# Memory keys of layer 1 moved into the first expert stage of a two-block fp32 transformer on one core, score copies put ahead of exponentials, key transposes put later

## The chip, the cores and the metric

The kernel runs on one core of one Trainium2 chip, in one launch. The metric is device time in microseconds (us); three runs of the kernel before gave a median of 1918.88 us (1917.76 to 1919.21). The engines are named as in the profile: PE (TensorE matmul), DVE (VectorE), ACT (ScalarE), POOL (GpSimd), SP (SyncE, which here starts nearly all weight transfers).

## The reference, cut to what matters

Everything is fp32. Two blocks of two layers each run one after the other. The first block works on 256 rows of width 1024:

```python
for layer in range(2):
    mix = even_mixer(x, ...) if layer % 2 == 0 else odd_mixer(x, ...)   # sliding window + spatial gate | pooling
    x = layer_norm(ALPHA * x + mix, ln1_g, ln1_b)
    x = layer_norm(ALPHA * x + memory_cross_attention(x, mem, xq, xkv, xo), ln2_g, ln2_b)
    x = layer_norm(ALPHA * x + grouped_moe(x, router_w, router_bias, e_gate, e_up, e_down), ln3_g, ln3_b)

def memory_cross_attention(x, mem, wq, wkv, wo):
    q = (x @ wq)...; kv = (mem @ wkv)...; k, v = kv[:, :, 0], kv[:, :, 1]     # mem: 256 rows, known from the start
    p = softmax(q k^T * X_HEAD_DIM ** -0.5); return (p v) @ wo

def grouped_moe(...):                     # 16 experts, two of them picked for each row
    he = silu(xt @ w_gate[e]) * (xt @ w_up[e]); y += combine[:, e:e+1] * (he @ w_down[e])
```

The second block (layers with adaptive norms, whose factors are rows `ada` made from a conditioning vector) has in layer 0 a differential attention (two softmaxes for each head, the second subtracted with a factor) and a SwiGLU network, and in layer 1 a grouped-query attention with normed and rotated queries and keys, and a second SwiGLU network.

The memory's keys and values for layer 1 (`mem @ wkv`) depend on nothing but inputs, so they can be formed at any time before the cross attention of layer 1.

## The kernel before, in words

**Arithmetic.** A large fp32 product is made from three matmuls on split operands. A weight chunk is 1 MB (128x2048). Its two halves of 128x1024 are each cast on ACT to `wh` (L253), and DVE or POOL subtracts to get the remainder `wl` (L254); `W.lo` names the engine of each half. The matmuls are hi x hi, lo x hi, hi x lo (L339 to L341, or L389 to L391 where the weight is the stationary operand). Expert weights (`gate`, `up`, `down`) are not split: they go raw into single matmuls (L1208, L1219).

**Weight stream.** The class `Stream` (object `W`) holds the planned order of all chunks. `load` starts transfers on SP's queue, in that order, as long as a buffer of some kind is free. The kinds and counts stand in `W.spare`: `raw`, and idle buffers of others (`w` is a pair of `wh`/`wl` buffers, `big` a large tile, `x`, `q`). `fill` gives a chunk to its user, and where it is not a raw one it writes the two casts and two subtractions at that place of the program. `ahead` calls `fill` for chunks further down the order, as far as free room goes, so the place of a cast on ACT is set by where `ahead` is called and by how many buffers there are.

**Order.** Each engine runs its instructions in the order in which the Python code emits them; there is no other scheduler. What is late on one engine holds what is emitted behind it.

**First expert stage, `moe(0)`.** The 16 experts run as eight pairs p. In step p the loop forms `gate` of pair p (four chunks), transposes the hidden rows of pair p-1 (`hidden_T`), adds the product of pair p-2 to its rows (`back`, matmuls `sct`, L1123 and L1124, operands `oh` and `ol`), forms `up` of pair p, calls the pair's hook, and runs `down` of pair p-1, whose product `po` is split on ACT and DVE into `oh` and `ol` (`out_split`). In step 8 the hook loads the transposed memory (`load_mem`, tile `memT`). After the stage, `last` adds the last pair, the layer norm is run, and in its gaps PE forms the four key chunks of layer 1 (`mem_k(1, j)`, tiles `memk` to `memK`, 48 matmuls of 128x256 each) and two halves of `ada` (`ada_go`). `W.spare["big"]` is 3 in the later pairs.

**Cross attention of layer 1.** The two value chunks of the first half (`mem_v(1, 0)`, 48 matmuls of 128x512 on `memv`) lie in the gaps of `w_out1`; those of the second half (`mem_v(1, 1)`) are the fill between the scores and the products of `cross`.

**Differential attention.** Each of 32 units (one head and one row tile) goes through `scores` (`dsc`, maximum `dmx` on DVE L1617 and L1618, two exponentials on ACT L1622), `combine` (DVE), `turn` (PE transposes L1639, ACT copy L1640) and `values` (PE `po` L1648). A `step(u)` runs the scores of unit u, one of its fills (half of a weight chunk's matmuls, `qkvp`), the `turn` of unit u-1, a second fill, and the values of unit u-1.

**Grouped-query attention.** `kv_tile` forms keys and values of a row tile (`gkv`), their square sums are turned to factors on POOL (`gkr`, L2004 and L345 to L356), `k_turn` scales on DVE (L2034) and transposes on PE (L2038), `q_half` forms queries (`gq`).

Of the kernel before, what the change touches and what calls it, by code (L numbers as in the profile page):

```python
# [213 lines left out]
def _build(nc, tc, A, out, ctx, order, plan):  # L214
# [601 lines left out]
    def mem_v(l, nh, vm):  # L816

        pss = [mm([128, 512], f"memv{t}") for t in range(2)]
        for i in range(2):
            ws = W.get(f"xv{l}", 2 * nh + i)  # L820
            W.ahead()
            tm_half(pss, range(2), fmt(memh), fmt(meml), ws, 4 * i, 8)
            if i == 1:
                for t in range(2):
                    S.copy(vm[:, t, nh * 512:nh * 512 + 512], pss[t])
            yield

    def idle():
        pass

    def mem_v_steps(l, vm):
        step = mem_v(l, 0, vm)
        return (lambda: next(step)), idle, (lambda: next(step))

    kT = big([128, 8, 256], F32, "memK")
# [96 lines left out]
    def cross(l, x, xh, xl, kT, vm, mid):  # L932
# [40 lines left out]
        for h in range(4):  # L973
            ps = mm([128, 2, 256], "xo", "B")
            for i in range(2):
                j = 2 * h + i
                for mc in range(2):
                    T.matmul(ps[:, i], vm[:, mc, j * 128:j * 128 + 128], PT[:, mc, h], start=mc == 0, stop=mc == 1)
            split(oh[:, 2 * h:2 * h + 2], ol[:, 2 * h:2 * h + 2], ps)
        return add_ln_router(l, x, f"xo{l}", fmt(oh), fmt(ol), f"ln2_{l}")  # L980

# [124 lines left out]
    def gated(pg, pu, cgc):  # L1106
        sg, hm = s2([128, 512], F32, "sg"), s2([128, 512], F32, "hm")
        S.activation(sg, pg, AF.Silu)
        V.scalar_tensor_tensor(hm, pu, cgc, sg, op0=OP.mult, op1=OP.mult)
        return hm  # L1110
# [82 lines left out]
    def moe(l, x, hooks):  # L1193
# [52 lines left out]
        for p in range(9):  # L1246
            if p == 1:
                W.spare["big"] = 1
            if p == 5:
                W.spare["big"] = 3  # L1250
            if p == 8:
                W.spare.update(w=0, big=0, x=1 - l, q=1 - l)
                W.lo = V, G
            if p < 8:
                pg = first(p, "gate")
            if p == 0:
                gains(0)
            else:
                hT[p - 1] = hidden_T(hm.pop(p - 1))
            if p > 1:  # L1260
                back(p - 2, 0)
            if p < 8:
                pu = first(p, "up")
                hm[p] = gated(pg, pu, cg[:, p:p + 1])
            if p == 0:
                ada_end()
                affine(0)
            if p == 1:
                affine(1)
                lists_T(0)  # L1270
            if p in (2, 3):
                gather_half(1, range(4 * p - 8, 4 * p - 4), "BB")
            if p == 3:
                gains(1)
                lists_T(1)
            if p > 1:
                back(p - 2, 1)
            if p == 4:
                beyond_lists()
            if p in hooks:  # L1280
                hooks[p]()
            if p:
                o[p - 1] = down(p - 1, hT.pop(p - 1))
# [2 lines left out]


    vm = big([128, 2, 1024], F32, "memV")
    x, xh, xl = add_ln(0, x, "w_out0", fmt(mh), fmt(ml), "ln1_0", *mem_v_steps(0, vm), mid=gate_T)
    W.spare.update(x=1, q=1)  # L1290
    W.whole, W.lo = 4, (V, G)
    x = cross(0, x, xh, xl, kT, vm, mem_v(0, 1, vm))

    def late_mem():
        nonlocal memh, meml, kT
        memh, meml = load_mem(G)
        yield
        kT = big([128, 8, 256], F32, "memK")
        for j in range(4):
            mem_k(1, j, kT)  # L1300
            if j % 2:
                ada_go()
            yield

    mk = late_mem()
    last, tt = moe(0, x, {8: lambda: next(mk)})
    W.whole = 4
    gb = ln_gb(2, "ln3_0")
    for t in range(2):
# [66 lines left out]
            V.scalar_tensor_tensor(ml[:, k], ps[:, i], sc, mh[:, k].bitcast(F32), op0=OP.mult, op1=OP.subtract)  # L1376
    ada_go()
    W.ahead()
    vm = big([128, 2, 1024], F32, "memV")
    W.spare["x"] = 0  # L1380
    x, xh, xl = add_ln(3, x, "w_out1", fmt(mh), fmt(ml), "ln1_1", *mem_v_steps(1, vm))
    W.spare.update(x=1, q=1)
    x = cross(1, x, xh, xl, kT, vm, mem_v(1, 1, vm))

    xs4 = [None] * 4
    order4 = (2, 3, 0, 1)
# [211 lines left out]
    class Unit:  # L1598
# [7 lines left out]
        def scores(self):  # L1606
# [5 lines left out]
            for m, ps in enumerate(pss):  # L1612
# [3 lines left out]
                mm3(ps, *q, *k, True, True)  # L1616
                V.tensor_reduce(mx[:, m:m + 1], ps, axis=AX, op=OP.max)  # L1617
            V.scalar_tensor_tensor(mx, mx, -1.0, rq, op0=OP.mult, op1=OP.mult)  # L1618
            self.P = []
            for m in range(2):  # L1620
                P = s2([128, 512], F32, "dP")
# [227 lines left out]
    def step(u, fills):  # L1849

        fills = list(fills)

        def fill():
            if fills:
                fills.pop(0)()

        if u < len(units):
            units[u].scores()
        out_step()
        if len(fills) > 1:  # L1860
            fill()
        if u:
            units[u - 1].turn()
        Qs[-1].scale(1)
        if u < len(units):
            units[u].combine()
        if 2 < u < 27:
            W.ahead(2)
        fill()
        Qs[-1].turn(1)  # L1870
        if u:
            units[u - 1].values()
# [180 lines left out]
    tabs = next(rope)  # L2053
    gate = [gate_row(1, 0, 0)]
    kv_tile(0)
    k_turn(1)
    kv_tile(1)
    W.limit = 2
    W.ahead()
    qs, qss, rq, pq = {}, {}, {}, {}  # L2060
# [28 lines left out]
    for i in range(2):  # L2089
        for t in range(2):  # L2090
            q_half(0, i, t)
            if i:
                q_heads(0, t)
        if i == 0:
            k_turn(0)
    for t in range(2):
        q_half(1, 0, t)
        q_turn(0, t)
    os_ = []
    Pg, PTs = {}, {}  # L2100
# [103 lines left out]
```

## Time and profile before

| | us |
|---|---|
| median of three runs | 1918.88 |
| the profiled execution, device time | 1917.83 |
| its span, first to last instruction | 1916.1 |
| PE busy in it | 1819.1 |
| DVE, ACT, POOL busy | 974.7, 703.8, 369.9 |
| mean granted TensorE clock | 0.984 of full speed |

The page's chain of work that ended last gives PE 59%, DMA 12%, DVE 9%, ACT 4% of the span. The stages differ: in the expert stages the DMA engines move about 421 GB/s with a busy share at or just over 1, elsewhere they move 56 to 320 GB/s. A busy time of PE in the expert stages counts matmuls that wait in the pipeline, so 19 of 20 us there do not say that PE is full.

### The profile page before, as it was taken

To read this page: it belongs to the slowest core of one execution; us is meant where nothing else is said; L and a number is where in the kernel's file an instruction comes from. 1 tells how busy PE (TensorE), PEld (TensorE's weight loads), DVE (VectorE), ACT (ScalarE), POOL (GpSimd) and SP (SyncE) were. 2 spreads that over 40 slices of the span, in tenths; PEclk is the share of its full clock that TensorE was granted. 3 is DMA by queue.
4 is the path that set the end of the run, shared out by engine and by line. 5 is a ranking of instruction groups with operands and counts; after the bars stand their busy time and mean duration, and the time that the engine had idled before them with its cause. 6 is when DMAs were issued, how large, how long until landed. Compare 5 with 4: busy or idle time off the path is not lost.

```text
span 1916.1 us, 25646 instructions
## 1 busy us (share of the span) xinstructions
PE 1819.1 (95%) x10038; PEld 1331.5 (69%) x10038; DVE 974.7 (51%) x1731; ACT 703.8 (37%) x1212; POOL 369.9 (19%) x594
## 2 busy tenths in 40 slices
PE   7999899999999899998899999999999998899998
PEld 6988634336788534335798876778888876559997
DVE  6884511115694421116666666534343466756665
ACT  6654312004554312103544543422322234545442
POOL 0003000003353000204575653100000024410000
PEclk9999899999999899999999999999999999999999
DMA  7546799999755899997511122342324223464552
GB/s 267 207 170 228 292 414 422 421 422 390 285 210 190 326 415 421 421 422 311 200 56 67 67 88 89 110 146 96 132 100 142 97 81 106 176 233 167 184 189 97
DMA packets 81587, 424.22 MB, mean 221 GB/s; under 512 B 9408, under 2 KB 9856, under 8 KB 49200
## 3 DMA queue, kind: packets, MB, share of 16 engines
q1 hardware_dynamic: 78768, 409.66, 56.2%
q0 software_dynamic: 2688, 12.81, 1.8%
q8 instruction: 83, 1.36, 0.3%
q14 instruction: 48, 0.39, 0.1%
HBM read 421.35 MB, written 1.08 MB: 220 GB/s over the span
## 4 chain that ended last, share of the span: by engine, by line
PE 59%; DMA 12%; DVE 9%; ACT 4%; issue 2%; POOL 2%; ACTq 0%; DVEq 0%; SPq 0%; POOLq 0%
DMA spare<-down 4%; DMA spare<-up 3%; PE fg L1702 3%; PE fu L1704 3%; PE fu L1703 3%; PE fu L1702 3%; PE fg L1703 3%; PE fg L1704 3%; PE fd L341 3%; PE fd L340 3%; PE fd L339 3%; PE pu L1208 3%; PE pg L1208 3%; DMA spare<-gate 3%; PE po L1219 2%
## 5 line engine op out<-in xcount | busy, mean ns | idle before, releaser
L253 ACT CAST wh<-raw 128x1024 fp32r<-128x1024 f32 (+1 forms) x248 | 248.5, 1047 | 131.0 <-PE fd L341 90.5
L254 DVE TENSOR_TENSOR wl<-raw,wh 128x1024 fp32r<-128x1024 f32 (+1 forms) x192 | 239.6, 1282 | 86.6 <-ACT wh L253 86.4
L254 POOL TENSOR_TENSOR wl<-raw,wh 128x1024 fp32r<-128x1024 f32 x56 | 144.5, 2594 | 252.8 <-ACT wh L253 241.8
L1703 PE MATMUL fg<-f,wh 128*128 128x256 f32 (+1 forms) x360 | 120.6, 335 | 2.6 <-DVE f L1435 2.4
L1702 PE MATMUL fg<-f,wh 128*128 128x256 f32 (+1 forms) x360 | 121.1, 336 | 1.7 <-DVE f L1434 1.4
L1702 PE MATMUL fu<-f,wh 128*128 128x256 f32 (+1 forms) x360 | 120.5, 335 | 0.0
L1703 PE MATMUL fu<-f,wh 128*128 128x256 f32 (+1 forms) x360 | 120.5, 335 | 0.0
L1704 PE MATMUL fu<-f,wl 128*128 128x256 f32 (+1 forms) x360 | 120.4, 334 | 0.0
L1704 PE MATMUL fg<-f,wl 128*128 128x256 f32 (+1 forms) x360 | 120.0, 333 | 0.0
L1219 PE MATMUL po<-spare,hT 128*64 128x512 f32 x456 | 109.1, 598 | 6.6 <-DMA spare<-down 2.3
L339 PE MATMUL qkvp<-wh,h 128*128 128x256 f32 x384 | 112.8, 294 | 0.5 <-ACT qsq L1560 0.5
L1721 DVE TENSOR_TENSOR fsg<-fu,fsg 128x512 f32<-128x512 f32 (+1 forms) x44 | 24.5, 558 | 171.1 <-PE fu L1704 169.2
L340 PE MATMUL qkvp<-wl,h 128*128 128x256 f32 x384 | 109.2, 284 | 1.8 <-POOL wl L254 1.8
L341 PE MATMUL qkvp<-wh,h 128*128 128x256 f32 x384 | 108.9, 284 | 0.0
L339 PE MATMUL fd<-wh,hid 128*128 128x512 f32 x264 | 103.0, 390 | 0.0
L340 PE MATMUL fd<-wl,hid 128*128 128x512 f32 x264 | 102.8, 389 | 0.0
L341 PE MATMUL fd<-wh,hid 128*128 128x512 f32 x264 | 102.7, 389 | 0.0
L1208 PE MATMUL pg<-spare,xg 128*64 128x512 f32 x360 | 87.1, 596 | 3.9 <-DMA spare<-gate 3.7
L253 ACT CAST hid<-fsg 128x512 fp32r<-128x512 f32 (+1 forms) x44 | 22.6, 513 | 183.5 <-DVE fsg L1721 183.5
L1208 PE MATMUL pu<-spare,xg 128*64 128x512 f32 x360 | 87.0, 597 | 0.4 <-DMA spare<-up 0.4
L253 ACT CAST oh<-po 128x512 fp32r<-128x512 f32 x32 | 18.7, 585 | 183.9 <-PE po L1219 183.9
L1219 PEld LDWEIGHTS po<-spare,hT 128*64 128x64 f32 x456 | 35.0, 136 | 73.1 <-issue 48.9
(667 smaller groups left out, 4272.2 us busy)
## 6 DMA issues: line engine op xcount, KB each, us to landing
spare<-down SPq DMA_DIRECT2D x94, 512.0 KB, 11.1
raw<-gu SPq DMA_DIRECT2D x42, 1024.0 KB, 4.9
spare<-up SPq DMA_DIRECT2D x80, 512.0 KB, 12.3
raw<-ada SPq DMA_DIRECT2D x36, 1024.0 KB, 5.1
spare<-gate SPq DMA_DIRECT2D x62, 512.0 KB, 11.1
raw<-dn SPq DMA_DIRECT2D x22, 1024.0 KB, 4.9
raw<-gate SPq DMA_DIRECT2D x19, 1024.0 KB, 12.3
raw<-up SPq DMA_DIRECT2D x19, 1024.0 KB, 13.5
```

The costliest lines, as they stand in the source:

```text
L253: (H.tensor_copy if H else S.copy)(hi, src)
L254: E.tensor_sub(lo, src, hi.bitcast(F32))
L339: T.matmul(ps, sh, mh, start=start, stop=False)
L340: T.matmul(ps, sh, ml, start=False, stop=False)
L341: T.matmul(ps, sl, mh, start=False, stop=stop_)
L1208: T.matmul(ps[64 * s:64 * s + 64], xg[h][k // 4][:, k % 4, 128 * b + 64 * s:128 * b + 64 * s + 64], w[s][:, kk * 512:kk * 512 + 512], star ...
L1219: T.matmul(po[nh][64 * s:64 * s + 64], hT[:, k, 64 * s:64 * s + 64], w[s][:, nh * 512:nh * 512 + 512], start=k == 0, stop=k == 3)
L1702: T.matmul(ps[:, cs], hi[:, c], h_, start=k == 0, stop=False)
L1703: T.matmul(ps[:, cs], hi[:, c], l_, start=False, stop=False)
L1704: T.matmul(ps[:, cs], lo[:, c], h_, start=False, stop=k == 7)
L1721: V.tensor_tensor(sg[:, :n], pss[1][:, :n], sg[:, :n], op=OP.mult)
```

## The change

It has three parts. First, the hook of steps 4 to 8 of `moe(0)` is now one step of `late_mem` each: the memory is loaded in step 4, the key tile taken in step 5, and key chunks 0, 1 and 2 formed in steps 6, 7 and 8; chunk 3 and both halves of `mem_v(1, 0)` follow after the stage, with `ada_go` beside them. `W.spare` has other counts there, remainders go to DVE (`W.lo = V, V`), and `W.fill(W.used + 1)` is called ahead of `gated` in the later steps and in step 8. The gaps of `w_out1` now take `mem_v(1, 1)`, the fill of the cross attention is four halves of `ada`, and since `ada` work is thereby earlier, the last four calls of `ada_go` (after `gout`) find nothing to do. Second, the exponentials leave `scores` and stand in a method `exps`, called behind the `turn` of the unit before. Third, `kv_tile(1)` runs ahead of `k_turn(1)`, and `k_turn(0)` behind `q_half(1, 0, 0)`.

```diff
     def mem_v_steps(l, vm):
-        step = mem_v(l, 0, vm)
+        step = mem_v(l, l, vm)
...
         for p in range(9):
             if p == 1:
                 W.spare["big"] = 1
+            if p == 4 and l == 0:
+                W.spare["w"], W.lo = 3, (V, V)
             if p == 5:
-                W.spare["big"] = 3
+                W.spare["big"] = 1 if l == 0 else 3
             if p == 8:
                 W.spare.update(w=0, big=0, x=1 - l, q=1 - l)
                 W.lo = V, G
+                if l == 0:
+                    W.fill(W.used + 1)
...
                 pu = first(p, "up")
+                if l == 0 and p > 4:
+                    W.fill(W.used + 1)
                 hm[p] = gated(pg, pu, cg[:, p:p + 1])
...
     def late_mem():
-        nonlocal memh, meml, kT
+        nonlocal memh, meml, kT, vm
         memh, meml = load_mem(G)
         yield
         kT = big([128, 8, 256], F32, "memK")
         for j in range(4):
+            yield
             mem_k(1, j, kT)
-            if j % 2:
-                ada_go()
+        yield
+        vm = [q4([128, 1024], F32, "memV") for _ in range(2)]
+        step = mem_v(1, 0, vm)
+        next(step)
+        yield
+        next(step)
+        for _ in range(3):
+            ada_go()
             yield

     mk = late_mem()
-    last, tt = moe(0, x, {8: lambda: next(mk)})
+    last, tt = moe(0, x, {p: lambda: next(mk) for p in range(4, 9)})
...
-    x = cross(1, x, xh, xl, kT, vm, mem_v(1, 1, vm))
+    def ada_fill():
+        for _ in range(2):
+            ada_go(2)
+            yield
+
+    x = cross(1, x, xh, xl, kT, vm, ada_fill())
...
             V.scalar_tensor_tensor(mx, mx, -1.0, rq, op0=OP.mult, op1=OP.mult)
+            self.pend = pss, mx, rq
+
+        def exps(self):
+            n, (pss, mx, rq) = 128 * self.nk, self.pend
             self.P = []
...
         if u:
             units[u - 1].turn()
+        if u < len(units):
+            units[u].exps()
         Qs[-1].scale(1)
...
     kv_tile(0)
+    kv_tile(1)
     k_turn(1)
-    kv_tile(1)
...
-        if i == 0:
-            k_turn(0)
     for t in range(2):
         q_half(1, 0, t)
+        if t == 0:
+            k_turn(0)
         q_turn(0, t)
```

**ACT at the end of the first expert stage.** This is ACT's queue before, from the product of pair 5 to the first key chunks (`wh<-spare` x6 are key chunks 0 to 2, two halves each; po_3690 is the product of pair 6, po_3755 that of pair 7).

```order
L253 CAST oh<-po_3567 128x512
L253 CAST oh<-po_3568 128x512
L1103 COPY hT<-tp 128x512
L1108 ACTIVATE sg<-pg 128x512
L253 CAST oh<-po_3690 128x512
L253 CAST oh<-po_3691 128x512
L1103 COPY hT<-tp 128x512
L253 CAST memTh<-spare 128x512 x4
L253 CAST oh<-po_3755 128x512
L253 CAST oh<-po_3756 128x512
L253 CAST wh<-spare 128x1024 x6
```

And this is the same queue of the changed kernel (po_3630 is the product of pair 5, po_3837 that of pair 6, po_3944 that of pair 7; `wh<-raw` x2 is key chunk 1, `wh<-spare` x4 are key chunks 2 and 3, the x2 below are a value chunk).

```order
L253 CAST oh<-po_3630 128x512
L253 CAST oh<-po_3631 128x512
L1103 COPY hT<-tp 128x512
L253 CAST wh<-raw 128x1024 x2
L1108 ACTIVATE sg<-pg 128x512
L253 CAST wh<-spare 128x1024 x4
L814 COPY memK<-memk 128x512
L253 CAST oh<-po_3837 128x512
L253 CAST oh<-po_3838 128x512
L1103 COPY hT<-tp 128x512
L253 CAST wh<-spare 128x1024 x2
L814 COPY memK<-memk 128x512
```

The casts of key chunks 2 and 3 now stand ahead of the evacuation of pair 6's product and of the copy of pair 7's hidden rows; before, no cast of a later weight stood ahead of them.

**SP at the same place.** SP's queue of the changed kernel, from key chunk 1 to key chunk 3 (a row of 128x1024 is half a chunk).

```order
L294 DMA raw<-xk 128x2048
L291 DMA spare<-down 128x1024 x4
L294 DMA spare<-down 128x2048
L291 DMA spare<-down 128x1024 x2
L291 DMA spare<-xk 128x1024 x2
L291 DMA spare<-down 128x1024 x2
L294 DMA raw<-down 128x2048 x2
L291 DMA spare<-down 128x1024 x2
L291 DMA spare<-xk 128x1024 x2
```

Key chunk 1 is fetched ahead of the four `down` chunks of pair 6, key chunk 2 behind them, and key chunk 3 behind the four of pair 7.

**ACT in the differential attention.** Two units of a head's end before, where `osq` belongs to a finished head.

```order
L253 CAST wh<-raw 128x1024 x2
L1559 COPY qs<-qkvp 128x512
L1560 ACTIVATE qsq<-qkvp 128x512
L253 CAST dkT<-tp 128x2x256
L1661 ACTIVATE osq<-os 128x512
L1622 ACTIVATE dP,dsum<-dsc,dmx,drq 128x512 x2
L1640 COPY dP<-tp 128x512
```

The changed kernel there (the same instructions have other line numbers).

```order
L253 CAST wh<-raw 128x1024 x2
L1578 COPY qs<-qkvp 128x512
L1579 ACTIVATE qsq<-qkvp 128x512
L253 CAST dkT<-tp 128x2x256
L1684 ACTIVATE osq<-os 128x512
L1663 COPY dP<-tp 128x512
L1645 ACTIVATE dP,dsum<-dsc,dmx,drq 128x512 x2
```

The copy of the unit before stands ahead of the exponentials of this unit; all else keeps its place.

**DVE in the grouped-query attention.** DVE's queue before, around the scaling of the last keys (`gks`; `wl` are remainders of query weights, `gqs` a query tile).

```order
L1491 TENSOR_TENSOR gks<-gks,tb 128x512
L1492 TENSOR_TENSOR gks<-gks,rot 128x512
L254 TENSOR_TENSOR wl<-raw,wh 128x1024 x2
L2034 TENSOR_TENSOR gks<-gks,gkr 128x512
L254 TENSOR_TENSOR gkT<-tp,gkT 128x2x256
L254 TENSOR_TENSOR wl<-raw,wh 128x1024
L1489 TENSOR_TENSOR rot<-gqs,tb 128x8x32 x2
```

DVE's queue of the changed kernel from the scaling of the other pair of key tiles on.

```order
L2059 TENSOR_TENSOR gks<-gks,gkr 128x512
L2069 SCALAR_TENSOR_TENSOR gkT<-tp,prm,gkT 128x2x256
L254 TENSOR_TENSOR wl<-raw,wh 128x1024 x3
L1508 TENSOR_TENSOR rot<-gqs,tb 128x8x32 x2
L1510 TENSOR_TENSOR gqs<-gqs,tb 128x512
L1511 TENSOR_TENSOR gqs<-gqs,rot 128x512
L1508 TENSOR_TENSOR rot<-gqs,tb 128x8x32 x2
L1510 TENSOR_TENSOR gqs<-gqs,tb 128x512
L1511 TENSOR_TENSOR gqs<-gqs,rot 128x512
L254 TENSOR_TENSOR wl<-raw,wh 128x1024
L2059 TENSOR_TENSOR gks<-gks,gkr 128x512
L254 TENSOR_TENSOR gkT<-tp,gkT 128x2x256
```

The last scaling of keys moved behind the remainders of the query weights and behind the rotation of two query tiles.

## Rows read from the trace of the kernel before

**Rows 1.** Stretches of 20 us: span, busy us (x) of PE, PEld, DVE, ACT, POOL, PEclk, DMA, GB/s
```profile
430.00:450.00 20.00, 19.12 (x73) 7.36 (x72) 5.79 (x9) 3.83 (x7) 4.98 (x4) 1.00 1.02 422
450.00:470.00 20.00, 18.84 (x125) 14.26 (x124) 14.69 (x30) 10.26 (x12) 11.64 (x5) 1.00 1.02 423
```
**Rows 2.** Timeline of PE, end of the first expert stage: start, us, instruction, idle and releaser
```profile
428.30 1.94 PE L1208 MATMUL pu<-raw,xg 128*64 128x512 f32 x8 [0.58 <-DMA raw<-up]
...
451.40 1.93 PE L1219 MATMUL po<-spare,hT 128*64 128x512 f32 x6 [0.17 <-DMA spare<-down]
453.27 0.50 PE L1123 MATMUL sct<-oh,PmT 128*128 128x512 f32 x1
```
**Rows 3.** Timeline of ACT, the same place
```profile
452.51 0.58 ACT L253 CAST oh<-po 128x512 fp32r<-128x512 f32 x1 [8.25 <-PE po L1219]
...
453.89 2.00 ACT L253 CAST wh<-spare 128x1024 fp32r<-128x1024 f32 x2
```
**Rows 4.** Timeline of PE, key chunk 0 after the stage
```profile
456.25 0.39 PE L391 MATMUL memk<-memTh,wl 128*128 128x256 f32 x1 [0.76 <-DVE wl L254]
456.47 0.28 PE L389 MATMUL memk<-memTh,wh 128*128 128x256 f32 x1
...
461.51 0.28 PE L389 MATMUL memk<-memTh,wh 128*128 128x256 f32 x1
```
**Rows 5.** Timeline of PE, value chunks in the cross attention of layer 1
```profile
596.00 0.39 PE L339 MATMUL memv<-wh,memTh 128*128 128x512 f32 x1
...
601.22 0.40 PE L341 MATMUL memv<-wh,memTl 128*128 128x512 f32 x1
601.45 1.04 PE L968 MATMUL tp<-cst,xP 128*128 128x128 f32 x8
```
**Rows 6.** Timeline of DVE there: the last probabilities
```profile
597.16 0.62 DVE L959 TENSOR_SCALAR xP<-xP,xsum 128x256 f32<-128x256 f32 x2
```
**Rows 7.** Waits of PE in the differential attention: engine, line, releaser, us, times, longest
```profile
PE po L1648 <- ACT dP L1640: 9.2, 6, 3.5
...
PE tp L1588 <- ACT dP L1640: 1.2, 1, 1.2
```
**Rows 8.** Waits of ACT there
```profile
ACT dP L1622 <- DVE dmx L1618: 82.2, 31, 4.7
```
**Rows 9.** Timeline of all engines there, the longest wait
```profile
1112.84 0.44 PE L1639 MATMUL tp<-cst,dP 128*128 128x128 f32 x2
```
**Rows 10.** Timeline of ACT there, the longest wait
```profile
1118.13 0.56 ACT L1622 ACTIVATE dP<-dsc,dmx,drq 128x256 f32<-128x256 f32 x1 [1.83 <-DVE dmx L1618]
...
1119.23 0.36 ACT L1640 COPY dP<-tp 128x256 f32<-128x256 f32 x1
```
**Rows 11.** Timeline of PE there, the longest wait
```profile
1119.64 0.71 PE L1648 MATMUL po<-dv,dP 128*128 128x128 f32 x4 [3.49 <-ACT dP L1640]
```
**Rows 12.** Timeline of PE, grouped-query attention: query matmuls and transposes of keys
```profile
1599.51 0.63 PE L2038 MATMUL tp<-cst,gks 128*128 128x128 f32 x4 [1.19 <-DVE gks L2034]
...
1610.68 0.39 PE L341 MATMUL gq<-wh,h 128*128 128x512 f32 x1
1616.31 1.12 PE L2038 MATMUL tp<-cst,gks 128*128 128x128 f32 x4 [5.25 <-DVE gks L2034]
...
1627.85 0.60 PE L2086 MATMUL tp<-cst,gqs 128*128 128x128 f32 x4
```
**Rows 13.** Timeline of POOL there: factors of the last keys, then remainders
```profile
1606.80 0.54 POOL L2004 TENSOR_SCALAR gkss<-gkss 128x4 f32<-128x4 f32 x1 [7.26 <-ACT gsq L2012]
...
1613.37 5.11 POOL L254 TENSOR_TENSOR wl<-raw,wh 128x1024 fp32r<-128x1024 f32 x2
```
**Rows 14.** The stretch behind that wait, columns as in rows 1
```profile
1616.00:1622.00 6.00, 5.69 (x16) 4.63 (x17) 2.17 (x3) 2.47 (x3) 4.46 (x2) 0.50 0.87 306
```
**Rows 15.** Timeline of PE after `gout`
```profile
1716.02 0.44 PE L1450 MATMUL tp<-cst,rtz 128*128 128x128 f32 x2 [2.00 <-ACT hf L1453]
...
1717.53 1.52 PE L570 MATMUL ada<-spare,csil 128*32 128x512 f32 x8
```

More of the change, by code (lines that the diff above doesn't have):

```diff
@@ L824, in mem_v @@
                 for t in range(2):
-                    S.copy(vm[:, t, nh * 512:nh * 512 + 512], pss[t])
+                    S.copy(vm[t][:, nh * 512:nh * 512 + 512], pss[t])
             yield
@@ L977, in cross @@
                 for mc in range(2):
-                    T.matmul(ps[:, i], vm[:, mc, j * 128:j * 128 + 128], PT[:, mc, h], start=mc == 0, stop=mc == 1)
+                    T.matmul(ps[:, i], vm[mc][:, j * 128:j * 128 + 128], PT[:, mc, h], start=mc == 0, stop=mc == 1)
             split(oh[:, 2 * h:2 * h + 2], ol[:, 2 * h:2 * h + 2], ps)
@@ L1288, in _build @@
     vm = big([128, 2, 1024], F32, "memV")
+    vm = vm[:, 0], vm[:, 1]
     x, xh, xl = add_ln(0, x, "w_out0", fmt(mh), fmt(ml), "ln1_0", *mem_v_steps(0, vm), mid=gate_T)
@@ L1378, in _build @@
     W.ahead()
-    vm = big([128, 2, 1024], F32, "memV")
     W.spare["x"] = 0
```

## Prediction

> **What bounds the kernel now.** I read the page's slices first, then stretches of 20 us, then PE's timeline where the change acts, and the waits by engine. The reader is to see three situations. In the first expert stage the transfers bound: 430 to 450 us and 450 to 470 us move 422 and 423 GB/s [rows 1], and PE ends its chunks by waiting for DMA (`up` at 428.30, `down` at 451.40) [rows 2]. A chunk of 1 MB (1.049 million bytes) takes 1.049 / 422 = 2.49 us. Behind the stage, from 453.27, PE bounds: the key matmuls follow each other without a hole after one wait of 0.76 [rows 4]. In the two attentions PE bounds too, broken by a few waits for ACT and DVE [rows 7, 12]. So PE work that goes into the expert stage is cheap only if it delays neither the transfers nor the chain PE, ACT, PE that each pair needs.
>
> **Part 1, the expert stage: +26 us, and 1.5 for the clock.** Transfers first. The memory was fetched inside the stage before as well. New ahead of the last `down` chunk are key chunks 0, 1 and 2: 3 x 2.49 = 7.5 us, so it lands at 451.4 + 7.5 = 458.9, and key chunk 3, which SP issues behind it, at 461.4.
>
> Now ACT. Its queue, shown with the change, has the casts of key chunks 2 and 3 ahead of `oh<-po` of pair 6 and ahead of the copy of pair 7's hidden rows. An engine that runs in order can evacuate pair 6 only when key chunk 3 is there. Before, ACT took a pair's product at once: it had idled 8.25 us at 452.51 [rows 3]. In the trace ACT is seen to hold a ready copy behind a late instruction: the transposes for the copy L1640 were done at 1113.28, and the copy ran at 1119.23, behind exponentials that waited for `dmx` [rows 9, 10].
>
> The Trainium skill (TensorE: Matmul & The Clock Gate, section "Architectural detail: the array is 16× 32×32, not 1× 128×128") states that ACT and DVE are strict FIFO; the trace agrees (5.95 us for the ready copy just named). If ACT could overtake, this part would be rival A below; that it can't is what the sum stands on.
>
> The new end: chunk 3's first half lands about 460.2 and its second at 461.4; the last cast (1.0 us for a half, 2.00 for two [rows 3]) ends at 462.4, the copy of key chunk 1 and two evacuations (0.58 each [rows 3]) at 464.0; PE has had nothing to do since about 451: pair 6's last `down` chunk lands at 458.9 - 5 x 2.49 = 446.4, key chunk 1 stood ahead of that pair's matmuls, and only the transposes of pair 7's hidden rows follow. So some 12 us of PE idle. Then, in order: `sct` of pair 6, eight matmuls of 128x512, at the pace of the value matmuls of that width (24 in 5.45 us [rows 5]) 1.8 us; key chunk 2, where 42 matmuls go from 456.47 to 461.51, 0.12 us each [rows 4], so 48 in 5.8 us; four `down` chunks that have all landed, eight matmuls each; eight of one chunk show 1.94 with the modelled end of the last [rows 2], without it about 1.75, so 7.0 us. That is 464.0 + 1.8 + 5.8 + 7.0 = 478.6 against 453.27 [rows 2]: +25.3, with small waits +26. It would be at least +13.5, as PE needs the last `down` chunk, key chunk 2 and `sct` in any case (458.9 + 1.75 for it, and 6 of what stood ahead and waited with it, 466.7), and at most +31 if PE's clock is low for half of what follows.
>
> A wait of 5.25 us [rows 12] was followed by 6 us at a granted clock of 0.50, the lower level of 1.2 GHz [rows 14]. I add 1.5 for the same thing after 12 us of idle, between nothing and 3.
>
> The Trainium skill (the same page, section "Loop structure matters more than you think") names a loop that waits for DMA between its matmuls as one that loses the clock. This case's trace agrees: 0.50 behind a wait of 5.25 us [rows 12, 14], there a wait for DVE. By that rule the term would be its upper end, 3.
>
> **Part 1, behind the stage: -7 us.** PE's dense stretch loses three key chunks (3 x 5.8 = 17.4) and the wait of 0.76 [rows 4], and gains two value halves. A value half is 24 matmuls; 24 of them run from 596.00 to 601.45 [rows 5], 5.45 us, so +10.9. Sum -7.3, with a little given back for layer norm steps that now have less cover. Between -9 and -4.
>
> **Part 1, cross attention of layer 1 and the `ada` work: -2.5 us.** The fill of 48 value matmuls (10.9 us, ending at 601.45 [rows 5]) becomes four `ada` halves at about 1 us each. The last probabilities are ready at 597.16 + 0.62 = 597.78 [rows 6], so PE can gain at most 601.45 - 597.78 = 3.7; `ada` also waits for an ACT copy behind the exponentials, so I take -1.5, between -3.7 and +1.5 (PE idles there, which can cost clock). After `gout`, two `ada` steps of some 2 and 3 us go; the first lies beside the 2.00 us wait for `hf` at 1716.02 and the second just ahead of the last transposes [rows 15]. I take -1, between -3 and +2.
>
> **Part 2, differential attention: -7 us.** ACT's exponentials wait 31 times for `dmx`, 82.2 us in all [rows 8], and PE waits for the copy behind them 9.2 us in 6 places and 1.2 in one [rows 7]. In the longest, the exponentials start at 1118.13, the copy at 1119.23, `po` at 1119.64 after 3.49 us [rows 10, 11]. With the copy first it runs as soon as `osq` is done (before 1117), so nearly all of this wait goes. The sum of these waits is 10.4, and clock lost behind some of them comes on top. Against it: in steps with one fill the copy comes ahead of exponentials for nothing, and exponentials that were not waiting come 0.36 to 0.59 later, with `combine` and the transposes behind them. What is late next is `dfc` on DVE, then the copy of the following unit. I take two thirds, -7; between -13 and -2.
>
> **Part 3, grouped-query attention: -6.5 us.** Gone are the waits of 1.19 and 5.25 [rows 12] and the half clock behind the second, which lasted 6 us [rows 14]. What is late next: the query matmuls reach the second half of the next query weight, whose remainder POOL makes behind the `gkr` chain (from 1606.80 to 1613.37, 6.6 us, then 5.11 for two [rows 13]). The chain starts some 1.2 earlier, so the remainder is there at about 1612.2 + 2.4 = 1614.6, when PE has waited from about 1612: 2.6 us. From the last `gq` before the wait to the first query transpose took 1627.85 - 1610.68 = 17.2 [rows 12]; now 36 matmuls at about 0.23 (8.2), the key transposes (0.8) and 2.6 of wait, 11.6. So -5.6 - 1.2 = -6.8, of which I keep 6.5; between -3 (if the new wait costs clock as the old one did) and -9 (if POOL is in time).
>
> **Sum.** 26 + 1.5 - 7 - 1.5 - 1 - 7 - 6.5 = +4.5 us on the profiled execution's 1917.83, which is 1922.3. That execution lies 1.05 under the median of the runs shown; the median plus 4.5 is 1923.4. I say 1923.
>
> **The rivals.** *A, the casts don't hold the pair* (chunk 3 early enough, or PE later than I think, so that most of the 12 us lie beside work). Then the stage ends 13.5 later instead of 26, and without the clock's 1.5 the sum is -9.5: 1909. For it: PE follows the transfers in this stage [rows 2], so when it arrives at pair 6 is worked out here and not read. Against it: the order of ACT's queue and the rate of 422 GB/s leave no place for chunk 3 before 461.
>
> *B, slower by much.* Mechanism: the stall as forecast, and the attentions give half: exponentials pushed behind copies make `combine` and the next scores late, and the POOL remainder in part 3 takes the place of the wait removed, clock included. Parts 2 and 3 then give -3 and -3, and the fill of the cross attention gives nothing: 26 + 1.5 - 7 - 1 - 3 - 3 = +13.5, 1932. For it: DVE's `dmx` is late 31 times [rows 8], and a chain through DVE, not the copy, may be what sets each step. It decides once parts 2 and 3 together give less than about 9. Against it: the waits for the copy stand in the trace by name [rows 7].
>
> *C, the attentions give all they have* (-13 and -9) with the stall as forecast: -4, 1915.
>
> **How the numbers follow.** My forecast 0.45, with its own range of 1917 to 1929; A 0.28; B 0.17; C 0.10. A measurement of this kernel tells a change from none at about 0.2%, 3.8 us, so faster means under 1915.1 and slower over 1922.7. The forecast gives 0.05 faster, 0.17 same, 0.23 slower; A 0.25 and 0.03 same; B slower; C half faster, half same. Together faster 0.35, same 0.25, slower 0.40. The range 1905 to 1934 takes in A and B with some of their bounds and leaves out about 2 in 10, at their far ends.
>
> **What would show it.** Right: a hole of 8 to 14 us in PE between the transposes of pair 7's hidden rows and `sct` of pair 6, named as a wait for `oh` on ACT, with ACT waiting for a transfer of `xk`; the stage's last `sct` of pair 7 about 25 us later; no PE wait on the copy in the differential attention over 2 us; a wait of 2 to 3 us of PE on POOL's remainder in part 3 in place of 5.25. Wrong: PE busy through 450 to 464, or `oh` of pair 6 cast before key chunk 3 has landed (then A); or PE waits on `dP` of the same sum as before (then B).

## The result, and the profile after

The changed kernel takes 1943.51 us (median of 4 runs, 1939.93 to 1944.73), against 1918.32 of the kernel before beside it: a ratio of 1.013 (95% interval 1.0116 to 1.0144), 25 us slower. The forecast was 1923 with a range to 1934, so it was too low. The profiled execution took 1939.93 us, 22.1 more than the one before. Its busy times:

```profile
PE 1821.0 (94%) x10038; PEld 1337.3 (69%) x10038; DVE 977.7 (50%) x1735; ACT 705.6 (36%) x1212; POOL 360.6 (19%) x590
```

PE's work is the same (1821.0 us against 1819.1, the same 10038 matmuls). What grew is the time in which PE waits. The waits of PE, longest sums first (engine, line, releaser, us in total, times, longest):

```profile
PE adat L581 <- ACT adar L576: 12.3, 3, 4.6
PE sct L1123 <- ACT oh L253: 11.2, 1, 11.2
...
PE tp L2063 <- DVE gks L2059: 6.5, 2, 3.3
PE gT L603 <- DVE ada L586: 5.7, 3, 3.3
...
PE ada L570 <- DVE h1l L254: 3.2, 1, 3.2
```

The second line is the forecast stall. Waits for `adar` were there before too (4.5 us, two times), and the prediction named one more in the cross attention; the waits for `gks`, 6.4 before, were forecast to go; those for `ada` (`gT`) and for `h1l` (0.8 before) were not forecast. Where they act is seen when the same matmul is found in both traces and its starts are subtracted (the lag; the step is its change):

| a matmul of | before | after | lag | step since the row above, forecast for it |
|---|---|---|---|---|
| `sct` of pair 7, end of the first expert stage | 453.27 | 479.87 | +26.6 | +26.6, forecast +27.5 |
| `w_in` of layer 1 | 484.02 | 503.27 | +19.2 | -7.4, forecast -7 |
| `pool`, behind `w_in` | 509.51 | 532.75 | +23.2 | +4.0, none |
| router scores behind the cross attention | 637.22 | 662.70 | +25.5 | +2.2, forecast -1.5 |
| first scores of the differential attention | 918.50 | 948.21 | +29.7 | +4.2, none |
| `dout`, behind its last unit | 1165.01 | 1188.80 | +23.8 | -5.9, forecast -7 |
| the queries (`gq`, 63rd of 96), behind both key transposes of part 3 | 1628.75 | 1652.55 | +23.8 | 0, forecast -6.5 |
| the second network, near its start (`fg`) | 1729.84 | 1752.18 | +22.3 | -1.5, forecast -1 |

**The stall.** PE's timeline of the changed kernel at the end of the stage (start, us, instruction, idle and releaser):

```profile
443.25 7.09 PE L1219 MATMUL po<-spare,hT 128*64 128x512 f32 x32
450.27 0.66 PE L1101 MATMUL tp<-cst,hm 128*128 128x128 f32 x4
462.09 0.80 PE L1123 MATMUL sct<-oh,PmT 128*128 128x512 f32 x1 [11.16 <-ACT oh L253]
...
472.85 1.94 PE L1219 MATMUL po<-spare,hT 128*64 128x512 f32 x8
```

and ACT's beside it:

```profile
447.65 1.05 ACT L253 CAST wh<-spare 128x1024 fp32r<-128x1024 f32 x1 [0.21 <-DMA spare<-xk]
458.81 1.05 ACT L253 CAST wh<-spare 128x1024 fp32r<-128x1024 f32 x1 [10.11 <-DMA spare<-xk]
460.02 1.05 ACT L253 CAST wh<-spare 128x1024 fp32r<-128x1024 f32 x1 [0.16 <-DMA spare<-xk]
...
461.45 1.08 ACT L253 CAST oh<-po 128x512 fp32r<-128x512 f32 x2
```

Pair 6's product was complete at about 450. ACT waited 10.11 us for the transfer of key chunk 3, and only then evacuated it; before, ACT had taken such a product at once [rows 3]. Behind the wait PE runs at the lower clock of 1.2 GHz, as it did behind the wait of the grouped-query attention [rows 14] (span, PE, PEld, DVE, ACT, POOL busy us, PEclk, DMA share, GB/s):

```profile
462.00:468.00 6.00, 5.82 (x17) 4.63 (x18) 5.22 (x8) 2.37 (x5) 0.00 (x0) 0.50 0.79 255
```

The eight matmuls of `sct` take 4.0 us there, where the prediction had 1.8.

**Part 3.** PE's two transposes of keys in the changed kernel, to be read against [rows 12]:

```profile
1630.70 0.63 PE L2063 MATMUL tp<-cst,gks 128*128 128x128 f32 x4 [3.14 <-DVE gks L2059]
...
1649.92 1.12 PE L2063 MATMUL tp<-cst,gks 128*128 128x128 f32 x4 [3.35 <-DVE gks L2059]
```

DVE at the same places:

```profile
1628.01 0.49 DVE L1508 TENSOR_TENSOR rot<-gks,tb 128x128 f32<-128x128 f32 x2 [4.94 <-ACT gks L2035]
...
1629.87 0.68 DVE L2059 TENSOR_TENSOR gks<-gks,gkr 128x512 f32<-128x512 f32 x1
...
1634.91 6.76 DVE L254 TENSOR_TENSOR wl<-raw,wh 128x1024 fp32r<-128x1024 f32 x2 [0.67 <-ACT wh L253]
1641.80 2.75 DVE L1508 TENSOR_TENSOR rot<-gqs,tb 128x256 f32<-128x256 f32 x2
...
1648.04 1.22 DVE L254 TENSOR_TENSOR wl<-raw,wh 128x1024 fp32r<-128x1024 f32 x1
1649.18 0.68 DVE L2059 TENSOR_TENSOR gks<-gks,gkr 128x512 f32<-128x512 f32 x1
```

and POOL:

```profile
1634.85 9.08 POOL L254 TENSOR_TENSOR wl<-raw,wh 128x1024 fp32r<-128x1024 f32 x3
```

The factors were ready before (POOL made the last of them at 1634.9, and the second scaling ran at 1649.18), but the scaling is emitted behind other work of DVE. Ahead of the first stand rotations that waited 4.94 us for ACT's copy of PE's newest product. Ahead of the second DVE is busy without a hole from 1634.91, and part of that time is POOL's doing: beside POOL's three remainders, two of DVE's take 6.76 us and two rotations 2.75, where they take 2.35 and 0.75 with POOL quiet (see the query remainders on DVE, below). The waits of 1.19 and 5.25 became 3.14 and 3.35. PE's clock is still at 0.51 from 1651 to 1656, where the table has its row: at the last of the 96 query matmuls the lag is +25.4, so part 3 gave nothing here or cost up to 1.6.

**The rest.** Four more waits of PE, from its timeline, in the stretches of the table's third to fifth row:

```profile
518.04 1.06 PE L570 MATMUL ada<-spare,csil 128*32 128x512 f32 x8 [3.16 <-DVE h1l L254]
...
621.32 0.79 PE L581 MATMUL adat<-cst,adar 128*128 128x128 f32 x4 [4.56 <-ACT adar L576]
...
635.10 1.99 PE L978 MATMUL xo<-xPT,memV 128*128 128x256 f32 x8 [1.51 <-DVE xol L254]
...
942.41 0.27 PE L603 MATMUL gT<-cst,ada 128*16 128x128 f32 x1 [3.30 <-DVE ada L586]
```

The first was 0.76 before:

```profile
496.41 1.07 PE L570 MATMUL ada<-raw,csil 128*32 128x512 f32 x8 [0.76 <-DVE h1l L254]
```

So it grew by 2.4, and from 519.3 to 522.7 the granted clock is 0.50, which by my estimate is another 1.7: the step of 4.0.

The second is the new fill of the cross attention: it waits for ACT's copy of its own row behind the exponentials. It lies where the value matmuls were before, and costs little in the end: the lag is +23.7 at the product behind it (`xo`, 604.44 before, 628.14 after), 0.5 over that of `pool`. The rest of the step of 2.2 is the third wait. ACT after:

```profile
628.83 3.89 ACT L253 CAST wh<-spare 128x1024 fp32r<-128x1024 f32 x4
632.62 1.60 ACT L253 CAST xoh<-xo 128x512 fp32r<-128x512 f32 x3
```

and before:

```profile
606.47 0.58 ACT L253 CAST xoh<-xo 128x512 fp32r<-128x512 f32 x1 [1.25 <-PE xo L978]
```

The casts of two chunks of the output weight ran from 596.82 to 600.7 before, under the value matmuls; with the other fill they have come to stand ahead of the evacuation (`xoh`) of the product, as in the stall, though here they wait for no transfer. The fourth wait ends a row of `ada`. Since `ada` work came earlier, the row ends here, ahead of the first scores; before, it ended inside the differential attention, where its operand was ready:

```profile
1009.39 0.27 PE L603 MATMUL gT<-cst,ada 128*16 128x128 f32 x1
```

### The profile page after: what moved, and what is told of

The parts are those of the page before. It is cut to its first block, busy times and chain, and to the rows that moved or that the text cites. A ratio compares the mean times of both kernels' runs of the same rounds, so it can differ in the third digit from the quotient of the medians.

```text
span 1938.0 us, 25609 instructions
## 1 busy us (share of the span) xinstructions
PE 1821.0 (94%) x10038; PEld 1337.3 (69%) x10038; DVE 977.7 (50%) x1735; ACT 705.6 (36%) x1212; POOL 360.6 (19%) x590
## 5 line engine op out<-in xcount | busy, mean ns | idle before, releaser
L253 ACT CAST wh<-raw 128x1024 fp32r<-128x1024 f32 (+1 forms) x258 | 258.8, 1048 | 155.7 <-PE fd L341 90.2
L254 DVE TENSOR_TENSOR wl<-raw,wh 128x1024 fp32r<-128x1024 f32 (+1 forms) x199 | 246.4, 1273 | 98.7 <-ACT wh L253 98.6
L254 POOL TENSOR_TENSOR wl<-raw,wh 128x1024 fp32r<-128x1024 f32 x59 | 153.9, 2622 | 251.5 <-ACT wh L253 232.6
L1219 PE MATMUL po<-spare,hT 128*64 128x512 f32 x432 | 98.8, 597 | 5.5 <-PEq L1132 4.0
L339 PEld LDWEIGHTS qkvp<-wh,h 128*128 128x128 f32 x384 | 74.1, 193 | 4.5 <-ACT qsq L1579 1.6
L1725 PEld LDWEIGHTS fg<-f,wh 128*128 128x128 f32 x360 | 69.1, 192 | 11.1 <-DVE f L1453 1.8
```

Source lines behind the costliest of these rows:

```text
L253: (H.tensor_copy if H else S.copy)(hi, src)
L254: E.tensor_sub(lo, src, hi.bitcast(F32))
L339: T.matmul(ps, sh, mh, start=start, stop=False)
L1219: T.matmul(po[nh][64 * s:64 * s + 64], hT[:, k, 64 * s:64 * s + 64], w[s][:, nh * 512:nh * 512 + 512], start=k == 0, stop=k == 3)
L1725: T.matmul(ps[:, cs], hi[:, c], h_, start=k == 0, stop=False)
```

## The experiments

Ratios are to runs of the kernel before, taken beside each version on the same chip, with the 95% interval. Different versions were in part measured on different chips, so a difference between two of them is given by the ratios too, where it is not the one of the medians.

**Part 2 alone.** The edit is the two hunks of part 2 on the kernel before. 

> The kernel before with part 2 alone (copies ahead of exponentials). Theory: part 2 does in the changed kernel what it was meant to (the lag against before falls from 29.5 to 23.7 us between 1010 and 1165 us), so alone it gives -5 to -7: about 1912 us, and no wait of PE for the copy over 2 us. Rival: that fall is a given-back wait of the earlier parts (ada rows, clock) and the copies gain nothing: 1917 to 1920 us.

 Measured 1910.71 us, ratio 0.9966 (0.9954 to 0.9979), and no wait of PE for the copy is left among the first seven. The first theory holds: part 2 is worth 6.5 us by the ratio, 7.8 by the medians.

**Part 3 alone.** 

> The kernel before with part 3 alone (key transposes later). Theory: the waits of 1.19 and 5.25 us become two waits of about 3.3 us each, since DVE scales the keys behind rotations that were emitted earlier: 1916 to 1920 us, no change to measure. Rival: part 3 alone gives the 6.5 us that I forecast, and in the changed kernel something of part 1 (ada work that came earlier) took it: about 1912 us.

 Measured 1919.28, ratio 1.0002 (0.9991 to 1.0013), with these waits of PE in that stretch:

```profile
PE tp L2038 <- DVE gks L2034: 8.1, 2, 5.0
```

So part 3 gives nothing by itself; nothing of part 1 took its gain. The two waits sum to 8.1 here (3.1 and 5.0, not twice 3.3 as expected), 6.5 in the changed kernel.

**Part 1 alone.** 

> The kernel before with part 1 alone. Theory: all of the loss is in part 1: +26.6 at the stage's end, -7.5 behind it, then new waits (+3 in w_in, +2 in the cross attention, +3 ahead of the differential attention), -1 after gout: 1943 to 1949 us, 4 to 7 more than the changed kernel. Rival: parts 2 and 3 together cost as much as they gain: within 2 us of the changed kernel, 1941 to 1945.

 Measured 1947.37, ratio 1.0157 (1.0144 to 1.0170). It lies inside the 1943 to 1949 expected, and over the changed kernel by 3.9 (medians) or 5.2 (ratios) where 4 to 7 was expected; the rival's 1941 to 1945 is missed. The three parts add up: 1.0157 x 0.9966 x 1.0002 = 1.0124, where 1.013 was measured.

**ACT's order mended.** The changed kernel with

```diff
+            if p == 7 and l == 0:
+                W.limit = 1
...
+        W.limit = 2
         W.ahead()
         return lambda t, *tags: back(7, t, *tags), tt
```

> The changed kernel with W.limit = 1 in the last two steps of the first expert stage (2 again at its end), so that the casts of key chunk 3 no longer stand ahead of pair 6's product on ACT. Theory: the wait of 11.2 us for oh goes, the stage's last sct of pair 7 starts near 467 instead of 479.9, and the kernel gains 11 to 14: 1930 to 1933 us. Rival: the transfers and PE's own work set the stage's end anyway, the wait turns up elsewhere: under 4 us gained, 1940 or more.

 Measured 1926.78, ratio 1.0059 (1.0044 to 1.0074): less than the changed kernel by 16.7 (medians), 13.6 (ratios) or 14.1 (profiled executions), so about the 11 to 14 expected. ACT and PE now:

```profile
449.16 0.58 ACT L253 CAST oh<-po 128x512 fp32r<-128x512 f32 x1 [0.38 <-PE po L1219]
449.99 0.59 ACT L253 CAST oh<-po 128x512 fp32r<-128x512 f32 x1 [0.25 <-PE po L1219]
...
458.52 2.23 ACT L253 CAST wh<-spare 128x1024 fp32r<-128x1024 f32 x2 [7.37 <-DMA spare<-xk]
```

```profile
463.67 1.89 PE L1219 MATMUL po<-spare,hT 128*64 128x512 f32 x8
465.48 0.50 PE L1123 MATMUL sct<-oh,PmT 128*128 128x512 f32 x1
```

The cast of key chunk 3 stands behind the evacuation and runs when it did (458.52, against 458.81), the stage ends at 465.48 instead of 479.87, and the cause of the stall is shown. It is still 12.2 later than before [rows 2], or 13.6 counted from the stage's first `gate` matmul, which came 1.4 earlier in this trace: the 13.5 that I had given as the least.

**Values and `ada` rows put back.** The same, with the value chunks in `w_out1` and in the cross attention and two `ada` calls behind the stage, as in the kernel before. 

> Keys in the expert stage with W.limit = 1 as in the run before (1926.78), but value chunks and ada rows where the kernel before has them (values in w_out1 and in the cross attention, two ada halves behind the stage, the last ada rows after gout); parts 2 and 3 as in the changed kernel. Theory: the moved ada rows and the missing fill cost 5 to 8 (cross attention +2, ahead of the differential attention +3, w_in +3), of which -1 after gout and some uncovered layer norm steps come back: 1920 to 1925 us, and the waits adat <- adar in the cross attention and gT <- ada ahead of the differential attention go. Rival: where values and ada stand makes no difference: 1926 to 1929.

 Measured 1918.8, ratio 1.0007 (0.9996 to 1.0018): 8.0 less than with them moved (10.0 by the ratios), a little under the 1920 expected. In the stretch from 560 to 960 PE's wait for `adar` is now 2.2 us where the changed kernel has 8.4, and the wait for `gT` is not among the first seven. So the moved fills cost about as much as their waits say; which of the three (values, fill, rows) cost how much was not run apart. But parts 2 and 3 are in this kernel, worth 6.5 and nothing, so keys in the stage still cost about 8. PE's waits from 464 to 510:

```profile
PE tp L433 <- DVE ln_0tt L417: 3.4, 1, 3.4
PE ada L570 <- DVE h1l L254: 3.4, 1, 3.4
```

The lag against before is +13.8 at the stage's end, +0.7 at the first `w_in` and +6.9 at `pool`: 13.1 of the keys' 17.4 come back behind the stage, and 6.2 are lost again in `w_in`.

**Part 3 with the scaling early.** On the kernel before: `k_turn` is cut in two, and only its PE half is late.

```diff
+    def k_scale(xc):
         k = ks[xc].rearrange("p t h d -> p (t h) d")
         V.tensor_tensor(k, k, kr[xc]...)
+    def k_turn(xc):
...
     kv_tile(0)
-    k_turn(1)
+    k_scale(1)
     kv_tile(1)
+    k_turn(1)
...
         if i == 0:
-            k_turn(0)
+            k_scale(0)
     for t in range(2):
         q_half(1, 0, t)
+        if t == 0:
+            k_turn(0)
```

> The kernel before with part 3 in another form: DVE's scaling of the keys is emitted where k_turn stood before, and only PE's transposes (and the split behind them) are late. Theory: in part 3 the waits moved because the scaling was emitted behind rotations on DVE; with the scaling early both waits go: 5 to 8 us less than before, 1911 to 1914, against no change for part 3 as it was. Rival: POOL's remainder of the next query weight is late next, as the prediction had it, and a wait of 2 to 5 us takes their place: 1915 to 1918.

 Measured 1914.09, ratio 0.9976 (0.9965 to 0.9986), a gain of 4.6 us by the ratio, 3.5 by the medians. Both waits for `gks` are gone, and POOL's remainder, which I had forecast as what is late next, is now there:

```profile
PE gq L340 <- POOL wl L254: 2.9, 1, 2.9
```

Both readings had a part: the theory for the cause, the rival for what follows.

**Parts 2 and 3 together, without part 1.** 

> The kernel before with part 2 and with the split form of part 3, without part 1. Theory: the gains add up, -6.5 (part 2 alone was 1910.71 against 1918.49) and -5 to -8: 1904 to 1908 us. Rival: the second gives nothing: 1910 to 1912.

 Measured 1909.15, ratio 0.9950 (0.9937 to 0.9963). The product of the two ratios (0.9966 x 0.9976 = 0.9942) lies within its interval; the time lies just over the range expected.

**Key chunks a step earlier.** The changed kernel with key chunks 0 to 2 in steps 5 to 7 and no casts ahead there. 

> The changed kernel with key chunks 0 to 2 formed one step earlier (steps 5 to 7 of the stage, the tile kT taken in step 5) and their casts emitted only by the fill ahead of gated (W.limit = 0 in steps 5 to 7), none in step 8. Theory: with W.limit = 1 the stage ended at 465.5 because key chunks 1 and 2 stand in PE's queue ahead of the last two down products, where PE has no slack left; one step earlier one of them lies in the slack: the end near 460 to 462, that is the three transfers of 2.49 over 453.3, and 1921 to 1924 us. Rival: PE has no slack in the earlier steps either and each key chunk costs its 5.8 us: the end at 465 to 470, 1926 to 1931.

 Measured 1929.99, ratio 1.0058 (1.0044 to 1.0073), no better than with W.limit = 1. The stage ends at 464.32:

```profile
436.87 1.94 PE L1208 MATMUL pu<-raw,xg 128*64 128x512 f32 x8 [0.53 <-DMA raw<-up]
...
447.43 7.09 PE L1219 MATMUL po<-spare,hT 128*64 128x512 f32 x32
...
464.32 0.50 PE L1123 MATMUL sct<-oh,PmT 128*128 128x512 f32 x1
```

From the last wait for a transfer PE does `up`, key chunk 2, and two `down` products with no wait over 0.8 us, so the last key chunk still lies in a tail that PE bounds. My 460 to 462 missed that; the rival's reading is the nearer one.

**Row operations on POOL.** The kernel with values put back (1918.8), `ln_rows` behind the stage on POOL. 

> The kernel with keys in the stage, W.limit = 1 and values and ada as before (1918.8), with the four row operations of the layer norm behind the stage (L422, L423: scale and shift of the rows, 9.4 us of DVE) on POOL. Theory: what that kernel still loses against part 2 alone is DVE's work of the layer norm and the remainders, which lay under the key matmuls before and is now late for h1l in w_in (wait 3.4 us, and half clock behind it); with 9.4 us less on DVE the wait goes: 3 to 6 us less, 1913 to 1916. Rival: the wait is set by PE's and ACT's order or by the transfers and stays, or POOL delays the remainders it makes: 1917 to 1921.

 Measured 1926.55, ratio 1.0052 (1.0037 to 1.0066): 7.7 slower (8.6 by the ratios). My theory's remedy failed. DVE there:

```profile
485.73 2.57 DVE L438 CAST ln_0h<-lnf 128x512 fp32r<-128x512 f32 x1
...
497.19 0.41 DVE L438 CAST ln_0h<-lnf 128x512 fp32r<-128x512 f32 x1
```

and POOL:

```profile
485.34 2.68 POOL L423 TENSOR_TENSOR ln_0y<-ln_0y,ln_0gb 128x1024 f32<-128x1024 f32 x1
487.98 2.54 POOL L422 TENSOR_TENSOR ln_0y<-ln_0tt,ln_0gb 128x1024 f32<-128x1024 f32 x1
```

A DVE cast of 0.41 us takes 2.57 to 2.59 while POOL works, each ending 0.3 us behind one of POOL's.

**Query remainders on DVE.** Parts 2 and 3 as in the run of 1909.15, with `W.lo = V, V` from the fill of the first query weight to the end of the `q_half` calls. 

> The kernel with part 2 and the split form of part 3 (1909.15), with the remainders of the query weights on DVE instead of half of them on POOL. Theory: the one wait left there, PE for POOL's remainder behind the gkr chain (2.9 us), goes: 1905 to 1907 us. Rival: four remainders on DVE (1.22 each) delay the rotation of the queries, and as much is lost: 1908 to 1911.

 Measured 1903.19, ratio 0.9930 (0.9917 to 0.9943): 6.0 less than with POOL (3.8 by the ratios), more than the 2.9 of the wait that went. DVE's rotation of the query tile with POOL's remainders beside it (the run of 1909.15), and here:

```profile
1615.77 2.94 DVE L1489 TENSOR_TENSOR rot<-gqs,tb 128x256 f32<-128x256 f32 x2
```

```profile
1610.06 2.35 DVE L254 TENSOR_TENSOR wl<-raw,wh 128x1024 fp32r<-128x1024 f32 x2
1612.33 0.75 DVE L1489 TENSOR_TENSOR rot<-gqs,tb 128x256 f32<-128x256 f32 x2
```

With POOL quiet DVE is sooner done although it makes all the remainders. This is the fastest version run, and it beats both kernels.

**The same with keys in the stage.** 

> Keys in the stage with W.limit = 1, values and ada as before, row operations on POOL, part 2, and the split form of part 3 with query remainders on DVE. Theory: with the three causes away (ACT's order, moved values and ada, DVE behind the stage) the keys in the stage are worth what PE's balance says, 17.4 less 12.2 for the stage's later end: 3 to 5 less than the same kernel without them: 1901 to 1904 us. Rival: keys in the stage gain nothing even so: within 2 us of the kernel without them, or above.

 Measured 1917.6, ratio 1.0003 (0.9991 to 1.0015): the rival. Keys, with the row operations on POOL, cost 14 us against the run of 1903.19; of these some 8 may be POOL's, if they cost here what they cost in the run of 1926.55. The same kernel with the row operations on DVE was not run.

**Remainders behind the stage on DVE, with and without keys.** `W.lo = V, V` from the last step of the stage to the end of `w_in`. 

> The kernel with keys in the stage, W.limit = 1 and values and ada as before (1918.8), with the remainders of all weights from the last step of the stage to the end of w_in on DVE (W.lo = V, V) instead of half on POOL. Theory: DVE's operations wait there for POOL's to end (0.42 us became 2.57 beside POOL's row operations; L422 and L423 took 3.3 to 3.4 instead of 1.22 beside POOL's remainders), so with POOL quiet DVE is done sooner although it has more to do: 3 to 7 us less, 1912 to 1916. Rival: DVE is simply full there, and the added remainders (1.22 each, seven or more) make it later: 1919 to 1925.

 Measured 1919.03, ratio 1.0011 (1.0001 to 1.0020), no change against 1918.8: the rival, if any. In its trace the wait for `h1l` is 0.8 instead of 3.4, and from the stage's end to `pool` it makes up 9.5 us where the kernel of 1918.8 makes up 6.9; but its stage ended 2.7 later, from a key chunk that landed late before this edit acts. So the remedy may be worth some 2 us that its runs do not show. 

> The kernel without keys in the stage, with part 2, the split form of part 3 and its remainders on DVE (1903.19), with the remainders behind the stage on DVE too. Theory: there the key matmuls cover DVE's work, PE waits only 0.76 and 1.0 us in that stretch, so nothing changes: 1902 to 1905. Rival: the engine is what counts, with or without keys: 1898 to 1901; or DVE, 14 us busy in 17 there, gets too full: 1906 or more.

 Measured 1906.82, ratio 0.9942 (0.9928 to 0.9956), 3.6 over the 1903.19 without it (2.3 by the ratios, whose intervals overlap). That DVE gets too full there, as I had expected, is not what its trace shows: PE's one new wait is 1.9 us for the cast of the first key chunk, and ACT waits 2.1 us there for the transfer. Why that came late stays open. In the kernel with keys (1919.03) two stretches show DVE full without POOL (columns as above):

```profile
476.00:485.00 9.00, 5.94 (x37) 3.38 (x39) 8.61 (x20) 3.51 (x9) 0.00 (x0) 0.84 0.98 371
485.00:497.00 12.00, 9.89 (x42) 7.51 (x35) 10.55 (x23) 7.37 (x16) 1.43 (x2) 0.69 0.70 273
```

POOL does next to nothing and DVE is full all the same (8.61 of 9 us, 10.55 of 12), while PE has holes: that the layer norm's chain and the remainders are what that stretch lasts is my reading.

## Why the prediction was wrong

- **The stage, +27.5 forecast, +26.6 measured.** Mechanism and place were right: ACT in order, behind key chunk 3. Making that order go took about 14 us off; the step was not the error. That the size fits so well is in part luck. PE started again at 462.09, 1.9 earlier than the 464.0 worked out, and the low clock behind the wait cost 3.1 (4.0 for `sct` instead of 1.8, and 0.9 in the key matmuls behind), twice the 1.5 added and at the upper end of 3 that was named beside it. Counted from the stage's first `gate` matmul, which came 1.1 earlier in this trace, the stage cost 27.7.
- **Behind the stage, -7.** Right at the first matmul of `w_in` (-7.4), but 4.0 came back in `w_in`. The step that failed was "with a little given back for layer norm steps that now have less cover". I priced only PE; the work under the cover is DVE's, and with less cover PE's wait for `h1l` went from 0.76 to 3.16, with low clock behind it. DVE was full there before as well, and PE's matmuls hid it (the kernel before, columns as above):

```profile
470.00:484.00 14.00, 14.00 (x119) 13.05 (x117) 13.51 (x18) 10.64 (x22) 4.63 (x2) 1.00 0.73 270
484.00:496.00 12.00, 11.65 (x56) 9.42 (x52) 11.93 (x7) 5.77 (x7) 7.53 (x5) 1.00 0.82 309
```

- **Cross attention and `ada`, -2.5.** The step "`ada` also waits for an ACT copy behind the exponentials, so I take -1.5" had a wait that came (4.56 us), but what it cost over the old fill was only 0.5; the other 1.7 of the +2.2 come with the wait of 1.51 behind the casts that now stand ahead of `xoh` on ACT, which the prediction did not look for there. That work moved earlier moves the gates that end a row was put at nothing: it is the wait of 3.30 ahead of the differential attention, in a step of +4.2. With fills and rows put back these waits go, and 8.0 us.
- **Part 2, -7.** Right: -5.9 in the trace, -6.5 alone (by the ratio of 0.9966). In the trace of part 2 alone the same two matmuls show -3.8, so the size is known to a few us only.
- **Part 3, -6.5.** Wrong: nothing. The step that failed was "what is late next": I named POOL's remainder, and did not follow DVE's queue, though the rows of it shown with the change put the scaling behind the rotation of two query tiles. DVE's order was late first; POOL's remainder came out, with 2.9 us, only when DVE's order was mended. I also had POOL only as a maker of remainders, and not as what slows DVE beside it (6.76 us for two remainders instead of 2.35).
- **The sum.** Forecast +4.5; the steps of the table add up to +22.2. The misses are 6.5 in part 3, 4.0 in `w_in`, 3.7 in the cross attention, 4.2 ahead of the differential attention, 1.1 in part 2, and -1.8 elsewhere (stage -0.9, behind it -0.4, the end -0.5): 17.7. The three other runs lie 2.5 to 4.8 above the profiled one, which the sum does not explain.
- **The rivals.** A did not occur, nor did C. B had the right sign, and its condition was met: parts 2 and 3 together gave less than 9. But its mechanism was another: part 2 gave nearly all it was priced at and part 3 nothing, where B had half of each, and B had no price for `w_in`, for the casts ahead of `xoh` or for the gate row; its 1932 was too low.

What stays open: keys in the stage cost about 8 us in the best form run with them, against the same parts without them. That PE waits for DVE behind the stage is shown; that DVE is the whole of it is argued, since neither remedy tried (row operations on POOL, remainders on DVE) made the kernel faster. The low clock behind these waits is part of it: 0.87 of full speed from 476 to 485 us and 0.76 from 497 to 511 in the kernel of 1918.8, 1.00 in the kernel before.

## What to carry to other kernels

A prefetch that also emits its cast puts that cast into an in-order queue, and a cast that waits for a transfer holds everything behind it, here for 10.11 us the evacuation on which the next step of PE hangs; look in the queue for what stands behind each new wait, and do so again wherever the fills were moved. When work is taken out of a gap, ask what ran under it: PE's matmuls left, and PE then waited for DVE's chain, hidden until then. When a step is put later, follow the queue of the engine that feeds it: only the PE half of `k_turn` had to be late, and with the DVE half left early the same idea gave 4 us instead of nothing.

## What the runs showed of the hardware

DVE and POOL hinder each other. Beside POOL's 128x1024 tensor operations, DVE's 128x512 cast took 2.57 us instead of 0.41, and scale and shift of a row tile 3.3 to 3.4 instead of 1.22. The other way round, one of POOL's small operations on the key factors, beside DVE's four remainders from 1602.72 to 1607.34 and 0.4 us behind them (run of 1903.19):

```profile
1604.08 1.07 POOL L355 TENSOR_SCALAR gkrh<-gkrh 128x4 f32<-128x4 f32 x1
...
1607.77 0.22 POOL L355 TENSOR_SCALAR gkrh<-gkrh 128x4 f32<-128x4 f32 x1
```

Behind waits of 3.2 to 11.2 us PE ran at the lower clock for a while (0.50 granted from 462 to 468 us and from 519.3 to 522.7, 0.83 in the mean of 938 to 948).

```profile
938.00:948.00 10.00, 6.01 (x34) 2.80 (x33) 5.55 (x17) 3.56 (x9) 4.12 (x15) 0.83 0.56 183
```
